# Bucket thresholds as bfloat16 masks added by TensorE and made one block later, a block-diagonal bias table, and row statistics of x from a token-major copy

## The chip, the cores and the metric

The kernel runs on one core of one Trainium2 chip. The metric is the device time of one execution, in microseconds. The engines are named as the profile names them: PE is TensorE and PEld its weight loads, DVE is VectorE, ACT is ScalarE, POOL is GpSimd, and SP is the queue engine that issues most of the DMAs.

## The reference, cut to what matters

A decoder trunk of two layers over 256 tokens with 1024 features, in float32. Layer 0 has differential attention with a relative bias, layer 1 latent attention; each has a gated FFN and a gated embedding behind it. The change touches the start of layer 0 alone:

```python
hn = rms_norm(h, attn_norm[0])                # h is x at this point
qkv = hn @ w_qkv
q = rms_norm(qkv[..., :qk_w].reshape(b, s, 8, 2, 64), q_gain)
k = rms_norm(qkv[..., qk_w:2 * qk_w].reshape(b, s, 8, 2, 64), k_gain)
...
n = max(pos_q - pos_k, 0)
log_ratio = log(max(n, 1) / 16) / log(128 / 16)
bucket = where(n < 16, n, min(16 + int(log_ratio * 16), 31))
sc = where(causal, q @ k.T * scale + rel_bias_table[bucket], -1e30)
```

The bucket of a distance n is also min(n, 16) plus the number of fifteen thresholds that n reaches. The bias of a head is a lookup in a table of 32 buckets by 8 heads.

## The kernel before, in words

All activations are feature-major: a tile holds 128 features by 256 tokens. Every matmul of float32 operands is done as three products (`mm3`, L197 to L199) of a high half and a low half. A weight unit of 128x1024 is loaded into the ring `st` (5 buffers), ScalarE casts it to the high half `wh` (L240), and VectorE or GpSimd in turn subtracts to get the low half `wl` (L241). The rings of `wh` and `wl` have 4 buffers each.

`proj_a(p)` makes q, k and v of two heads: three groups of 48 products, each with two weight units (`block`, called blocks 1 to 6 below for the two calls ahead of attention). Block 1 is `first_block`: it takes x and its weights in quarters as they land, and makes the halves of x times the norm gain (`hgH`, L637 and L639; `hgL`, L640) between its products. The norm of x itself is put in later: `epsx` adds up the squares of x over the features on ScalarE and GpSimd, `first_stats` has TensorE add them over the partitions (L301) and makes the mean `m` and its inverse root `xs["r"]`, which block 1's own normalization (`norm_block`, L342 to L353) needs.

`bias_prep` follows `first_stats` in the code, behind block 2. It builds the bias table three times in bfloat16, split so that the three add up (`tb`), in a 128x32 form with one 32x8 copy in each of four diagonal places (L401), and then the bucket index:

```python
V.tensor_scalar(bk, dist, 16.0, None, ALU.min)
for th in THRESH:
    V.scalar_tensor_tensor(bk, dist, float(th), bk, ALU.is_ge, ALU.add)
```

The index goes to memory as bfloat16 (`bkb` to `s`), and comes back as 24 loads that repeat rows of it over partitions (`oh`, L448). VectorE compares them with the partition's number (L456), and TensorE multiplies these one-hot rows with the table (`bias_mm`, 288 short products, L463). Attention starts behind that, woven with `proj_a(2)`, `proj_a(3)` and the output projection.

The order on each engine is not that of the code. The program is scheduled when it is built, by a model of time; each engine then runs its own list strictly in order and waits on semaphores. So are the loads on SP.

Of the kernel before, what the change touches and what calls it, by code (L numbers as in the profile page):

```python
# [9 lines left out]
F32 = mybir.dt.float32  # L10
# [9 lines left out]
P = 128  # L20
S = 256
# [22 lines left out]
C_LAM = 194  # L44
C_FREQ = 450
C_REL = 482
C_CONV = (490, 666)
NCONST = 842

def _out_order():  # L50
    cut = 14
# [41 lines left out]


@with_exitstack
def trunk(ctx, tc, xT, pT, pos, consts, grow, wall, out):
    nc = tc.nc
    V, A, G, T = nc.vector, nc.scalar, nc.gpsimd, nc.tensor

# [40 lines left out]
    def small(n, tag="s"):  # L140
        return sm.tile([P, 8], F32, tag=tag, name=tag, bufs=24)[:, :n]
# [161 lines left out]
        V.tensor_scalar(m, ps[:, :4].rearrange("p (a b) -> p a b", b=2)[:, :, 0], 1.0 / D, EPS, ALU.mult, ALU.add)  # L303
        return m

    def tok_stats(sq):
        m = tok_mean(sq)
        r = small(NT, "m")
        rsqrt_(r, m, NT)
        return m, r  # L310

    def rstd_diag(sq):
        m, r = tok_stats(sq)
        dg = d_tile(S)
        for t in range(NT):
            V.tensor_scalar(dg[:, t * P:(t + 1) * P], ident, r[:, t:t + 1], None, ALU.mult)
        return dg
# [71 lines left out]
    bst = {}  # L389

    def bias_prep():
        trel = col(C_REL, 8)
        tb = []
        rest = trel
        for i in range(3):
            bt = ap_.tile([P, 32], BF16, name=f"tb{i}")
            G.memset(bt, 0.0)
            q = ap_.tile([P, 8], BF16, name=f"tq{i}")
            V.tensor_copy(q, rest)
            for j in range(4):  # L400
                V.tensor_copy(bt[j * 32:(j + 1) * 32, j * 8:(j + 1) * 8], q[j * 32:(j + 1) * 32])  # L401
            tb.append(bt)
            if i < 2:
                nr = small(8)
                V.tensor_sub(nr, rest, q)
                rest = nr
        bi = ap_.tile([P, 1], F32, name="bi")
        bidx = ap_.tile([P, 1], I32, name="bidx")
        G.iota(bidx, pattern=[[0, 1]], base=0, channel_multiplier=1)
        V.tensor_scalar(bidx, bidx, 31, None, ALU.bitwise_and)  # L410
        V.tensor_copy(bi, bidx)
        V.tensor_copy(posf, posi)
        dist = e_tile()
        V.tensor_scalar(dist[:, :S], posf[:, :S], posf[:, S:S + 1], 0.0, ALU.subtract, ALU.max)
        V.tensor_scalar(dist[:, S:], posf[:, P:S], posf[:, S + 1:S + 2], 0.0, ALU.subtract, ALU.max)
        bk = e_tile()
        V.tensor_scalar(bk, dist, 16.0, None, ALU.min)
        for th in THRESH:
            V.scalar_tensor_tensor(bk, dist, float(th), bk, ALU.is_ge, ALU.add)
        bkb = ap_.tile([P, 384], BF16, name="bkb")  # L420
        V.tensor_copy(bkb, bk)
        s0 = dp.tile([P, S], BF16, name="s0")
        s1 = dp.tile([P, P], BF16, name="s1")
        nc.sync.dma_start(s0, bkb[:, :S])
        nc.sync.dma_start(s1, bkb[:, S:])
        bst["pcs"] = []
        later(LAG, lambda: bias_loads(s0, s1))
        bst["tb"], bst["bi"] = tb, bi
        ld = small(2)
        lscr = a_tile()  # L430
        for j in range(2):
            V.tensor_tensor_reduce(lscr[:, j * 64:(j + 1) * 64], col(C_LAM + 128 * j, 64),
                                   col(C_LAM + 128 * j + 64, 64), 1.0, 0.0, ALU.mult, ALU.add, ld[:, j:j + 1])
        le = small(2)
        A.activation(le, ld, AF.Exp)
        V.scalar_tensor_tensor(neglam, le[:, 1:2], -LAM_INIT, le[:, 0:1], ALU.add, ALU.subtract)
# [41 lines left out]
    def proj_a(p):  # L478
# [16 lines left out]
        for s in range(3):  # L495
# [8 lines left out]
            if p == 0 and s == 0:  # L504
                epsx()
            elif p == 0 and s == 1:
                first_stats()
                bias_prep()
            while "r" in xs and todo:
                post(*todo.pop(0))  # L510
# [114 lines left out]
                       lambda k: oL[(h0 + k) // 4][:, (h0 + k) % 4], post)  # L625

    xs = {}
    hgq = sumsq_begin()

    def get_first():  # L630

        for i in range(2):
            u = ring_pair()
            for j in range(4):
                k, q = 4 * i + j, slice(j * S, (j + 1) * S)
                if k % 2 == 0:
                    A.activation(hgH[:, k], hT[:, k], AF.Copy, scale=col(C_ATTN[0] + k))  # L637
                else:
                    V.tensor_scalar(hgH[:, k], hT[:, k], col(C_ATTN[0] + k), None, ALU.mult)  # L639
                V.scalar_tensor_tensor(hgL[:, k], hT[:, k], col(C_ATTN[0] + k), f(hgH[:, k]), ALU.mult, ALU.subtract)  # L640
                A.copy(u[0][:, q], first[i][:, q])  # L641
                V.tensor_sub(u[1][:, q], first[i][:, q], f(u[0][:, q]))
# [8 lines left out]
        return ps  # L651

    def epsx():
        for k in range(NK):
            sumsq_add(hgq, k)
        V.tensor_scalar(gq[:, 0:1], col(C_AQ), -SCALE_A, None, ALU.mult)
        V.tensor_scalar(gq[:, 1:2], col(C_QN), -SCALE_B, None, ALU.mult)
        V.tensor_scalar(gq[:, 2:3], col(C_ASUB), 1.0 - LAM_INIT, None, ALU.mult)

    def first_stats():  # L660
        m, xs["r"] = tok_stats(hgq)
        ep = cp.tile([P, 8], F32, name="epsx")
        V.tensor_scalar(ep.rearrange("p (t n) -> p t n", t=NT), m.unsqueeze(2).to_broadcast([P, NT, 4]), EPS,
                        None, ALU.mult)
# [487 lines left out]
def _layout(inp, np):  # L1152
# [96 lines left out]
    half = 32  # L1249
    arg = np.float32(-math.log(10000.0)) * np.arange(half, dtype=np.float32) * np.float32(2.0 / 64)  # L1250
    cst[:, C_FREQ:C_FREQ + half] = np.exp(arg.astype(np.float64)).astype(np.float32)
    cst[:, C_REL:C_REL + 8] = np.tile(f("rel_bias_table"), (4, 1))

    def featT(a):
        s, d = a.shape
        return np.ascontiguousarray(a.reshape(s, d // P, P).transpose(2, 1, 0))

    xT = featT(f("x")[0])
    pT = np.stack([featT(f("p")[l, 0]) for l in range(2)])
    pv = np.asarray(inp["positions"], dtype=np.int32)[0]  # L1260
    pos = np.zeros((P, S + NT), np.int32)
    pos[:, :S] = pv
    pos[:, S:] = pv.reshape(NT, P).T
    return {"in_x": xT, "in_p": pT, "in_pos": pos, "in_consts": cst, "in_grow": grow, "in_wall": wall}


# [16 lines left out]
```

## Time and profile before

| | |
|---|---|
| median of 3 runs | 793.84 us (792.4 to 794.16) |
| the profiled execution's own time | 794.75 us |
| its span, first to last instruction | 793.0 us |
| TensorE busy | 760.3 us, 96% |
| VectorE, ScalarE, GpSimd busy | 577.9, 481.6, 300.6 us |
| mean granted clock of TensorE | 0.983 of full speed |

Busy times overlap. The share of TensorE is a mean over the whole span; a stretch has to be looked at by itself to see whether TensorE or another engine sets the time there. Matmuls are pipelined, so a matmul's duration is longer than the step from one to the next.

### The profile page before, as it was taken

How to read it: one execution, taken by the hardware profiler on the slowest of the kernel's cores; microseconds unless marked ns; L12 is line 12 of the kernel's file. 1: busy time of each engine (PE TensorE's matmuls, PEld its weight loads, DVE VectorE, ACT ScalarE, POOL GpSimd, SP SyncE). 2: the span in 40 equal slices, each digit the busy share in tenths (PEclk: the TensorE clock that was granted, in tenths of full speed). 3: DMA queues.
4: the chain of work that ended last, by engine and by line, in shares of the span. 5: the costliest groups of instructions: out<-in, count | busy, mean ns of one | idle time of the engine just before them, and what ended most of it. 6: DMA issues, size and time to landing. Idle time of an engine off the chain costs nothing.

```text
span 793.0 us, 16490 instructions
## 1 busy us (share of the span) xinstructions
PE 760.3 (96%) x6384; PEld 747.9 (94%) x6384; DVE 577.9 (73%) x1158; ACT 481.6 (61%) x1039; POOL 300.6 (38%) x210
## 2 busy tenths in 40 slices
PE   6988999999999999998999899999899999999997
PEld 5877999999999999997989899999899999999997
DVE  7974888659987786547678987975558877775535
ACT  5334888567666665446866867664646666655443
POOL 5533456262333330235743746422433332301141
PEclk9989999999999999999999999999999999999999
DMA  7475345435666676555344333343455655565641
GB/s 289 158 193 185 110 132 173 133 110 184 181 191 187 188 229 206 188 167 174 112 160 136 106 107 94 99 131 108 157 157 181 194 178 181 177 194 183 185 130 54
DMA packets 37231, 126.91 MB, mean 160 GB/s; under 512 B 4640, under 2 KB 6176, under 8 KB 37152
## 3 DMA queue, kind: packets, MB, share of 16 engines
q1 hardware_dynamic: 36432, 125.32, 51.1%
q8 instruction: 50, 0.82, 0.4%
q10 hardware_dynamic: 720, 0.53, 0.2%
q14 instruction: 29, 0.24, 0.1%
HBM read 124.69 MB, written 1.15 MB: 159 GB/s over the span
## 4 chain that ended last, share of the span: by engine, by line
PE 83%; DVE 6%; issue 3%; POOL 3%; ACT 2%; DMA 2%; SPq 1%; POOLq 0%; DVEq 0%; ACTq 0%
PE pa L197 17%; PE pa L198 17%; PE pa L199 17%; PE pc L198 8%; PE pc L199 8%; PE pc L197 8%; POOL wl L241 2%; PE pb L198 1%; DVE wl L241 1%; PE pb L197 1%; PE pb L527 1%; PE pb L199 1%; PE pc L193 1%; POOL s L274 1%; PE pt L193 1%
## 5 line engine op out<-in xcount | busy, mean ns | idle before, releaser
L240 ACT CAST wh<-st 128x1024 fp32r<-128x1024 f32 x221 | 231.2, 1050 | 189.5 <-issue 70.4
L241 POOL TENSOR_TENSOR wl<-st,wh 128x1024 fp32r<-128x1024 f32 x74 | 178.4, 2411 | 240.8 <-ACT wh L240 229.4
L241 DVE TENSOR_TENSOR wl<-st,wh 128x1024 fp32r<-128x1024 f32 x147 | 189.8, 1292 | 84.3 <-ACT wh L240 83.9
L197 PE MATMUL pa<-hgH,wh 128*128 128x256 f32 x504 | 144.2, 286 | 2.2 <-ACT hgH L206 2.2
L198 PE MATMUL pa<-hgL,wh 128*128 128x256 f32 x504 | 144.2, 286 | 0.5 <-DVE hgL L207 0.3
L199 PE MATMUL pa<-hgH,wl 128*128 128x256 f32 x504 | 143.7, 285 | 0.0
L198 PE MATMUL pa<-wl,hgH 128*128 128x256 f32 x328 | 96.5, 295 | 9.5 <-DVE wl L241 6.1
L197 PEld LDWEIGHTS pa<-hgH,wh 128*128 128x128 f32 x504 | 97.9, 194 | 2.6 <-ACT hgH L206 2.6
L198 PEld LDWEIGHTS pa<-hgL,wh 128*128 128x128 f32 x504 | 97.9, 194 | 1.1 <-DVE hgL L207 1.1
L199 PEld LDWEIGHTS pa<-hgH,wl 128*128 128x128 f32 x504 | 98.0, 194 | 0.0
L197 PE MATMUL pa<-wh,hgH 128*128 128x256 f32 x328 | 95.8, 296 | 0.8 <-ACT wh L641 0.6
L199 PE MATMUL pa<-wh,hgL 128*128 128x256 f32 x328 | 95.2, 292 | 0.5 <-DVE hgL L204 0.5
L197 PE MATMUL pa<-og,wh 128*128 128x256 f32 x336 | 95.3, 287 | 0.0
L198 PE MATMUL pa<-og,wh 128*128 128x256 f32 x336 | 95.1, 284 | 0.0
L199 PE MATMUL pa<-og,wl 128*128 128x256 f32 x336 | 94.9, 283 | 0.0
L198 PE MATMUL pc<-hgL,wh 128*128 128x256 f32 x328 | 93.3, 285 | 0.6 <-DVE hgL L207 0.5
L197 PE MATMUL pc<-hgH,wh 128*128 128x256 f32 x328 | 93.5, 285 | 0.1
L199 PE MATMUL pc<-hgH,wl 128*128 128x256 f32 x328 | 93.0, 283 | 0.0
L296 POOL TENSOR_TENSOR ssq<-ssq,d 128x256 f32<-128x256 f32 x42 | 39.4, 937 | 136.5 <-ACT d L295 135.1
L198 PEld LDWEIGHTS pa<-wl,hgH 128*128 128x128 f32 x328 | 65.2, 199 | 11.1 <-DVE wl L241 6.9
L197 PEld LDWEIGHTS pa<-wh,hgH 128*128 128x128 f32 x328 | 64.4, 198 | 2.1 <-ACT wh L641 1.0
L274 POOL TENSOR_TENSOR s<-s,neghalf 128x4 f32<-128x4 f32 (+2 forms) x30 | 41.7, 1390 | 64.3 <-DVE s L345 46.1
(300 smaller groups left out, 1968.2 us busy)
## 6 DMA issues: line engine op xcount, KB each, us to landing
st<-in_wall SPq DMA_DIRECT2D x225, 512.0 KB, 3.6
oh<-s SPq DMA_DIRECT2D x24, 128.0 KB, 4.5
hT<-in_x SPq DMA_DIRECT2D x4, 256.0 KB, 5.3
st<-in_wall SPq DMA_DIRECT2D x4, 256.0 KB, 5.5
d<-in_p SPq DMA_DIRECT2D x2, 256.0 KB, 4.6
out_h<-hT SPq DMA_DIRECT2D x4, 128.0 KB, 1.9
out_h<-hT ACTq DMA_DIRECT2D x4, 128.0 KB, 2.0
grow<-in_grow SPq DMA_DIRECT2D x1, 384.0 KB, 6.1
```

Source lines behind the costliest of these rows:

```text
L193: T.transpose(o, i, ident)
L197: T.matmul(ps, lhsT=aH, rhs=bH, start=start, stop=False)
L198: T.matmul(ps, lhsT=aH, rhs=bL, start=False, stop=False)
L199: T.matmul(ps, lhsT=aL, rhs=bH, start=False, stop=stop)
L240: A.copy(hi, st)
L241: eng.tensor_sub(lo, st, f(hi))
L274: G.tensor_tensor(dst, src, neghalf[:, :n], ALU.pow)
L296: G.tensor_add(sq, sq, t)
L527: T.matmul(pss[e][:, a:b], lhsT=x[rows, j, t * P:(t + 1) * P], rhs=y[rows, j, :b - a], start=start, stop=stop)
```

## The change

Four edits at the start of layer 0:

1. The bucket index: the distance is kept in bfloat16, cut off at 128. Each threshold becomes a mask of zeros and ones in bfloat16 (ring `ge`, 4 buffers), and TensorE adds the masks up in PSUM by 16 products with an identity. ScalarE copies the sum out as the index.
2. `bias_prep` is called one block later, behind block 4 (`p == 1 and s == 0`).
3. The bias table comes from the host in its block-diagonal form of 32 columns, so that it is split by whole-tile casts and subtractions.
4. The squares of x are added up from a second copy of x, token-major (`xN`, two tiles of 512 KB through the ring `st`), by ScalarE's accumulating square. The eight squares, seven additions and the ones-product of the feature-major way go. All eight `hgH` scalings are ScalarE's now.

```diff
-    def tok_stats(sq):
-        m = tok_mean(sq)
-        r = small(NT, "m")
-        rsqrt_(r, m, NT)
-        return m, r
...
     def bias_prep():
-        trel = col(C_REL, 8)
         tb = []
-        rest = trel
+        rest = col(C_REL, 32)
         for i in range(3):
             bt = ap_.tile([P, 32], BF16, name=f"tb{i}")
-            G.memset(bt, 0.0)
-            q = ap_.tile([P, 8], BF16, name=f"tq{i}")
-            V.tensor_copy(q, rest)
-            for j in range(4):
-                V.tensor_copy(bt[j * 32:(j + 1) * 32, j * 8:(j + 1) * 8], q[j * 32:(j + 1) * 32])
+            V.tensor_copy(bt, rest)
             tb.append(bt)
             if i < 2:
-                nr = small(8)
-                V.tensor_sub(nr, rest, q)
+                nr = ap_.tile([P, 32], F32, name=f"tr{i}")
+                V.tensor_sub(nr, rest, bt)
                 rest = nr
...
-        dist = e_tile()
-        V.tensor_scalar(dist[:, :S], posf[:, :S], posf[:, S:S + 1], 0.0, ALU.subtract, ALU.max)
-        V.tensor_scalar(dist[:, S:], posf[:, P:S], posf[:, S + 1:S + 2], 0.0, ALU.subtract, ALU.max)
-        bk = e_tile()
-        V.tensor_scalar(bk, dist, 16.0, None, ALU.min)
-        for th in THRESH:
-            V.scalar_tensor_tensor(bk, dist, float(th), bk, ALU.is_ge, ALU.add)
+        identb = ap_.tile([P, P], BF16, name="identb")
+        V.tensor_copy(identb, ident)
+        dist = ap_.tile([P, 384], BF16, name="dist")
+        V.tensor_scalar(dist[:, :S], posf[:, :S], posf[:, S:S + 1], 128.0, ALU.subtract, ALU.min)
+        V.tensor_scalar(dist[:, S:], posf[:, P:S], posf[:, S + 1:S + 2], 128.0, ALU.subtract, ALU.min)
+        pb = bankB()
+        for j in range(len(THRESH) + 1):
+            ge = ap_.tile([P, 384], BF16, tag="ge", name="ge", bufs=4)
+            if j == 0:
+                V.tensor_scalar(ge, dist, 0.0, 16.0, ALU.max, ALU.min)
+            else:
+                V.tensor_scalar(ge, dist, float(THRESH[j - 1]), None, ALU.is_ge)
+            T.matmul(pb[:, :384], lhsT=identb, rhs=ge, start=j == 0, stop=j == len(THRESH))
         bkb = ap_.tile([P, 384], BF16, name="bkb")
-        V.tensor_copy(bkb, bk)
+        A.copy(bkb, pb[:, :384])
...
             elif p == 0 and s == 1:
                 first_stats()
+            elif p == 1 and s == 0:
                 bias_prep()
...
-                if k % 2 == 0:
-                    A.activation(hgH[:, k], hT[:, k], AF.Copy, scale=col(C_ATTN[0] + k))
-                else:
-                    V.tensor_scalar(hgH[:, k], hT[:, k], col(C_ATTN[0] + k), None, ALU.mult)
+                A.activation(hgH[:, k], hT[:, k], AF.Copy, scale=col(C_ATTN[0] + k))
...
     def epsx():
-        for k in range(NK):
-            sumsq_add(hgq, k)
...
     def first_stats():
-        m, xs["r"] = tok_stats(hgq)
+        xs["ss"] = small(NT, "m")
+        for t in range(NT):
+            xt = ring.tile([P, UNIT], F32, tag="st", name="st", bufs=BUF_ST)
+            nc.sync.dma_start(xt, xN[:, t])
+            A.activation(xt, xt, AF.Square, accum_out=xs["ss"][:, t:t + 1])
+        m, xs["r"] = small(NT, "m"), small(NT, "m")
+        V.tensor_scalar(m, xs["ss"], 1.0 / D, EPS, ALU.mult, ALU.add)
+        rsqrt_(xs["r"], m, NT)
```

VectorE between block 1's last low half and the fourth weight pair, before (`ex` is the distance or the running index, `wl` a low half of a weight unit, `tq` and `tb` the table):

```order
L663 TENSOR_SCALAR epsx<-m 128x8
L241 TENSOR_TENSOR wl<-st,wh 128x1024
L401 COPY tb_323<-tq_325 32x8 x4
...
L419 SCALAR_TENSOR_TENSOR ex<-ex 128x384
L343 TENSOR_REDUCE s<-d 128x8
L401 COPY tb_333<-tq_335 32x8 x4
L241 TENSOR_TENSOR wl<-st,wh 128x1024
...
L347 SCALAR_TENSOR_TENSOR s<-s,epsx 128x8
L419 SCALAR_TENSOR_TENSOR ex<-ex 128x384 x4
L241 TENSOR_TENSOR wl<-st,wh 128x1024
...
L353 TENSOR_TENSOR d<-pa,s 128x256 x2
```

And of the change, in the same place (`ge` is a mask):

```order
L338 TENSOR_REDUCE s<-d 128x8
L391 CAST tb_468<-tr_466 128x32
L415 TENSOR_SCALAR ge<-dist 128x384 x4
L241 TENSOR_TENSOR wl<-st,wh 128x1024
L415 TENSOR_SCALAR ge<-dist 128x384 x6
L659 TENSOR_SCALAR m<-m 128x2
L415 TENSOR_SCALAR ge<-dist 128x384 x2
L662 TENSOR_SCALAR epsx<-m 128x8
L342 SCALAR_TENSOR_TENSOR s<-s,epsx 128x8
L348 TENSOR_TENSOR d<-pa,s 128x256 x2
L241 TENSOR_TENSOR wl<-st,wh 128x1024
```

Although the code calls `bias_prep` a block later, the masks stand earlier: all sixteen are ahead of the second whole-unit low half, and the normalization of block 1 (L348) is one low half further ahead. TensorE, of the change, behind block 1 (its last product is the first row; `identb` is the identity):

```order
L199 MATMUL pa<-wh,hgL 128x256
L416 LDWEIGHTS identb
L416 MATMUL pb<-ge,identb 128x384
...
L197 MATMUL pa<-wh,hgH 128x256
...
L198 MATMUL pa<-wl,hgH 128x256
```

Four mask products stand behind block 1, four more behind block 2's first product, four behind its next twelve, and the last four behind its other 35. Before, none of these rows was there. ScalarE behind its first-block casts, before and of the change:

```order
L641 CAST wh<-st 128x256 x2
L240 CAST wh<-st 128x1024
L342 ACTIVATE d<-pa 128x256 x2
L240 CAST wh<-st 128x1024 x2
L435 ACTIVATE s<-s 128x2
```

```order
L635 CAST wh<-st 128x256 x2
L337 ACTIVATE d<-pa 128x256 x2
L240 CAST wh<-st 128x1024 x2
L657 ACTIVATE st,m<-st 128x1024 x2
L240 CAST wh<-st 128x1024 x2
L337 ACTIVATE d<-pa 128x512
L418 CAST bkb<-pb 128x384
```

Block 2's first cast went behind the squares of block 1's result, and the squares of x (L657) stand behind block 2's casts. SP's loads, as a difference:

```order
-L224 DMA st<-in_wall 128x1024 x4
-L669 DMA cst<-in_consts 128x352
-L817 DMA grow<-in_grow 128x768
-L224 DMA st<-in_wall 128x1024 x8
-L424 DMA s_369<-bkb 128x256
...
+L224 DMA st<-in_wall 128x1024 x2
+L656 DMA st<-in_xn 128x1024 x2
...
+L224 DMA st<-in_wall 128x1024 x6
+L421 DMA s_532<-bkb 128x256
+L422 DMA s_533<-bkb 128x128
+L224 DMA st<-in_wall 128x1024 x2
+L445 DMA oh<-s_532 32x2048 x16
```

The copy of x came in ahead of the third block's weights, and the index leaves behind eight whole units, not twelve.

## Rows read from the trace of the kernel before

**Rows 1.** Busy us of each engine by stretch, granted clock, DMA share, GB/s

```profile
0.00:80.00 80.00, 64.47 (x673) 61.34 (x674) 59.41 (x109) 34.85 (x79) 35.26 (x37) 0.91 0.65 205
80.00:160.00 80.00, 79.11 (x669) 75.76 (x667) 63.72 (x177) 60.69 (x165) 36.00 (x22) 1.00 0.44 136
```

**Rows 2.** TensorE's timeline: start, duration, instruction, idle before it and what ended it

```profile
18.66 0.58 PE L198 MATMUL pa<-wl,hgH 128*128 128x256 f32 x1 [1.62 <-DVE wl L241]
...
27.49 0.39 PE L198 MATMUL pa<-wl,hgH 128*128 128x256 f32 x1 [1.34 <-DVE wl L241]
...
43.12 0.58 PE L198 MATMUL pa<-wl,hgH 128*128 128x256 f32 x1 [2.91 <-DVE wl L241]
...
58.63 0.63 PE L193 MATMUL pt<-ident,d 128*128 128x128 f32 x4 [0.73 <-DVE d L353]
...
66.91 1.61 PE L463 MATMUL pb<-tb,oh 128*128 128x32 bf16 x58 [1.95 <-issue]
...
72.83 1.15 PE L463 MATMUL pb<-tb,oh 128*128 128x32 bf16 x38 [1.78 <-issue]
```

**Rows 3.** TensorE's timeline: two neighbouring products at 43 us, two at 57 us

```profile
43.50 0.41 PE L199 MATMUL pa<-wh,hgL 128*128 128x256 f32 x1
43.71 0.41 PE L197 MATMUL pa<-wh,hgH 128*128 128x256 f32 x1
...
57.50 0.28 PE L198 MATMUL pa<-wl,hgH 128*128 128x256 f32 x1
57.62 0.28 PE L199 MATMUL pa<-wh,hgL 128*128 128x256 f32 x1
```

**Rows 4.** VectorE's timeline

```profile
18.52 2.33 DVE L401 COPY tb<-tq 32x8 bf16<-32x8 bf16 x1
...
30.27 3.43 DVE L241 TENSOR_TENSOR wl<-st,wh 128x1024 fp32r<-128x1024 f32 x1
...
38.61 3.32 DVE L419 SCALAR_TENSOR_TENSOR ex<-ex 128x384 f32<-128x384 f32 x3
```

**Rows 5.** GpSimd's timeline

```profile
18.45 2.38 POOL L241 TENSOR_TENSOR wl<-st,wh 128x1024 fp32r<-128x1024 f32 x1 [0.48 <-ACT wh L240]
...
28.13 1.94 POOL L274 TENSOR_TENSOR s<-s,neghalf 128x8 f32<-128x8 f32 x1 [2.15 <-DVE s L347]
30.04 2.57 POOL L241 TENSOR_TENSOR wl<-st,wh 128x1024 fp32r<-128x1024 f32 x1
37.94 2.39 POOL L241 TENSOR_TENSOR wl<-st,wh 128x1024 fp32r<-128x1024 f32 x1
```

**Rows 6.** Two lines of block 1: min/median/max in ns, first and last start

```profile
L640 DVE SCALAR_TENSOR_TENSOR hgL<-hT,cst,hgH x8: 473/480/981, 4.9 to 14.2; 128x256 fp32r<-128x256 f32 x8
...
L642 DVE TENSOR_TENSOR wl<-st,wh x8: 412/416/951, 5.7 to 15.3; 128x256 fp32r<-128x256 f32 x8
```

**Rows 7.** Groups by line, first 80 us: busy us, mean ns, idle before

```profile
L419 DVE SCALAR_TENSOR_TENSOR ex<-ex 128x384 f32<-128x384 f32 x15 | 9.9, 660 | 0.2
...
L456 DVE TENSOR_SCALAR oh<-oh,bi 128x2048 bf16<-128x2048 bf16 x6 | 7.1, 1189 | 5.3 <-DMA oh<-s 5.3
...
L296 POOL TENSOR_TENSOR ssq<-ssq,d 128x256 f32<-128x256 f32 x7 | 5.7, 817 | 4.6 <-ACT d L295 4.2
...
L343 DVE TENSOR_REDUCE s<-d 128x8 f32<-128x512 f32 x4 | 2.7, 674 | 0.0
```

**Rows 8.** ScalarE's timeline

```profile
11.06 0.70 ACT L641 CAST wh<-st 128x256 fp32r<-128x256 f32 x2
...
16.78 0.66 ACT L342 ACTIVATE d<-pa 128x256 f32<-128x256 f32 x2 [3.22 <-PE pa L199]
17.32 1.99 ACT L240 CAST wh<-st 128x1024 fp32r<-128x1024 f32 x2
```

**Rows 9.** Loads into `st`, first 50 us

```profile
DMA to landing us min/median/max: 3.3/4.4/6.9
```

**Rows 10.** SP's timeline: the loads of the one-hot rows

```profile
46.99 9.76 SPq L448 DMA_DIRECT2D oh<-s  x20
```

More of the change, by code (lines that the diff above doesn't have):

```diff
@@ L46 @@
 C_REL = 482
-C_CONV = (490, 666)
-NCONST = 842
+C_CONV = (514, 690)
+NCONST = 866
 def _out_order():
@@ L95, in trunk @@
 @with_exitstack
-def trunk(ctx, tc, xT, pT, pos, consts, grow, wall, out):
+def trunk(ctx, tc, xT, xN, pT, pos, consts, grow, wall, out):
     nc = tc.nc
@@ L304, in tok_mean, with rstd_diag @@
         return m
-    def tok_stats(sq):
-        m = tok_mean(sq)
-        r = small(NT, "m")
+    def rstd_diag(sq):
+        m, r = tok_mean(sq), small(NT, "m")
         rsqrt_(r, m, NT)
-        return m, r
-    def rstd_diag(sq):
-        m, r = tok_stats(sq)
         dg = d_tile(S)
@@ L627, in trunk @@
     xs = {}
-    hgq = sumsq_begin()
     def get_first():
@@ L1251, in _layout @@
     cst[:, C_FREQ:C_FREQ + half] = np.exp(arg.astype(np.float64)).astype(np.float32)
-    cst[:, C_REL:C_REL + 8] = np.tile(f("rel_bias_table"), (4, 1))
+    for j in range(4):
+        cst[j * 32:(j + 1) * 32, C_REL + j * 8:C_REL + (j + 1) * 8] = f("rel_bias_table")
     def featT(a):
@@ L1258, in _layout @@
     xT = featT(f("x")[0])
+    xN = np.ascontiguousarray(f("x")[0].reshape(NT, P, D).transpose(1, 0, 2))
     pT = np.stack([featT(f("p")[l, 0]) for l in range(2)])
@@ L1263, in _layout @@
     pos[:, S:] = pv.reshape(NT, P).T
-    return {"in_x": xT, "in_p": pT, "in_pos": pos, "in_consts": cst, "in_grow": grow, "in_wall": wall}
+    return {"in_x": xT, "in_xn": xN, "in_p": pT, "in_pos": pos, "in_consts": cst, "in_grow": grow, "in_wall": wall}
 def kernel(**inputs):
```

## Prediction

> **What bounds the kernel now.** I read the busy time by stretch first. TensorE is busy for 79.1 of 80 us after the first 80 us, but for only 64.5 of the first 80 [rows 1]. So the time is TensorE's, and an edit at the start is worth what it takes out of TensorE's holes there. Next I read TensorE's own timeline for the pieces with idle time ahead of them [rows 2]: 1.62 us before 18.66, 1.34 before 27.49, 2.91 before 43.12, 0.73 before 58.63, then 1.95 and 1.78 before 66.91 and 72.83. All but the last three end on a low half (`wl`) written by VectorE. The hole at 43 costs twice. Products then start every 0.21 us, where they start every 0.12 us at 57.5 [rows 3]: that is the lower of the clock's two levels, after TensorE had stood still. It lasts 29 products, so 29 x 0.09 = 2.7 us more.
>
> Why is VectorE late? Its timeline [rows 4] beside GpSimd's [rows 5]: at 18.52 a 32x8 copy takes 2.33 us, at 30.27 a low half takes 3.43 us, at 38.61 three threshold steps take 3.32. Each time a 128x1024 subtraction of GpSimd (2.4 us) is under way, and VectorE goes on when it ends. The rest is the sheer work ahead of the low halves: 15 threshold steps of 0.66 us, 9.9 us in all [rows 7], and the twelve small copies.
>
> Call the 48-product groups of TensorE blocks 1 to 6 (the two first weight pairs), and the weight units u0, u1, ... (two to a block). In [rows 2] block 2 starts at 18.66, block 3 at 27.49, and the transposes behind block 6 at 58.63.
>
> **Block 1.** The change takes eight squares from ScalarE, seven additions (5.7 us) from GpSimd [rows 7], and four scalings from VectorE, which ScalarE gets. Without those additions beside them the eight `hgL` and eight `wl` steps should run at their medians, 0.48 and 0.42 us, not at up to 0.98 and 0.95 [rows 6]. ScalarE ended its last first-block cast at 11.76 [rows 8], no load waited for there, and loses about as much as it gains, so it ends near 11.6 again. VectorE follows it by half a microsecond (12.1, where it was at 15.7: the last `wl` step starts at 15.3), and block 1 ends near 13.0 where it ended just ahead of the wait at 17.0.
>
> **Block 2.** In the new order ScalarE casts u2 and u3 only behind the squares of block 1: 13.0 + 0.55 + 1.0 + 1.0, so u2 is there at 14.6 and u3 at 15.6 [rows 8]. VectorE has meanwhile the reduction (0.67) [rows 7] and eight masks. A mask is a bfloat16 step of 384 columns, which the trace lacks. The one bfloat16 step that it has takes 1.19 us on the mean for 2048 columns [rows 7], with waits in it; by columns that is 0.22 us, and the threshold step that it replaces took 0.66. I take 0.2, nearer to the row of its own type. So u2's low half runs from 15.4 to 16.6 and block 2 starts there, 2 us earlier. The first eight mask products lie in TensorE's wait before it and cost nothing; without that wait they would cost 8 x 0.18 (384 columns at 0.12 us for 256 [rows 3]), 1.4 us. GpSimd's u3 comes right behind VectorE's u2 and holds VectorE to about 19.0; masks 9 to 12 follow, and TensorE waits for both near 20.
>
> **Block 3.** The statistics of x now come from two 512 KB loads and two squares of 128x1024 on ScalarE. I price a square as the cast of that shape, 1.0 us [rows 8] (bounds 1.0 and, with the accumulator read, 1.3): done near 18, hidden behind block 2. The loads stand third and fourth in SP's weight stream and take two of the five `st` buffers, so u4 is issued at 12.2, when u1's buffer is free, and lands 4.4 us later (3.3 to 6.9) [rows 9], at 16.6 to 19: still ahead of use. Behind a late copy of x ScalarE's casts of u4 and u5 would wait. The block-diagonal table is three casts and two subtractions of 32 columns in place of twelve copies, under half a microsecond in the same place, and its 24 more columns of constants are 12 KB. Then the last masks, the powers on GpSimd (the 128x8 one 1.94 us [rows 5]) to about 22.6, and there u5's half on GpSimd goes first (2.4), so that VectorE has u4's low half at 25.0 + 1.2. Block 3 starts at 26.3, 1.2 us earlier than before. The last four mask products and the first transposes end before that.
>
> **Blocks 3 to 6** are the large term. Before, they took 58.63 - 27.49 = 31.1 us. VectorE now has no threshold step left there, and the low halves of u6 and u8 fall due at 32 and 38 while VectorE can give them at 28 and 32. Products alone: 191 x 0.12 = 22.9, and 0.6 for one group of transposes, 23.5. That removes 7.6: the holes of 2.91 and 0.73, the 2.7 of clock, the rest smaller. The bucket index is ready near 26, where the threshold steps alone ended at 41.9 [rows 4]. SP then has u10 and u11, 20 loads of the one-hot rows, u12 and four more. These took 9.8 us to issue [rows 10], so they end near 41, before the transposes at 49.8; u12 is not needed before 52. What is queued behind the index on SP, u10 and u11, is due at 43.
>
> **The bias products and attention** stand in the same order as before, so I give them the same time. Sum: 1.2 + 7.6 = 8.8 us. The profiled execution took 794.75 (793.0 of it span), 0.91 above the median 793.84. So 785.95 in a like execution, and **785.0** as a median.
>
> [...] The rows above show VectorE held for as long as a subtraction of GpSimd lasts, by copies and two-input steps alike [rows 4, 5]. [...] With VectorE first at u2 the sum stands at 785.0; with GpSimd first it is the first rival's 786.4.
>
> **Rivals.** (1) *GpSimd first.* u2 and u3 are free for it within 0.2 us of each other. If GpSimd takes u3 at 15.4, VectorE's u2 ends at 19.0, block 2 starts no earlier than before, and block 3 at 27.7: 1.4 us more, 786.4. If TensorE then stands long enough for the slow products to come back as at 43, 2.7 more, 789.1. For it: the margin; against: VectorE's queue is back to back there. The same times result if a mask costs 0.66: 8 x 0.46 = 3.7, 788.7.
> (2) *The holes at 66.91 and 72.83 go too.* They end on nothing that the trace shows, in the middle of a run of short bias products. They are 3.7 us, and the slow products behind the second (9 x 0.09) 0.8: 780.5. For it: their place is not tied to any data. Against: the same short products run at the same rate, so I expect them again. [...]
> (3) *No change.* The time is given back in attention because VectorE or ScalarE bounds it: 793.8. Against: TensorE at 79.1 of 80 there, VectorE 63.7, ScalarE 60.7 [rows 1].
> (4) *Slower.* TensorE's queue is in order, and now holds four groups of four mask products among its own. If VectorE's masks wait for GpSimd at each group, a group costs 2.4 us of hole and 2.7 of slow clock, 5.1. Two groups take 10.2 and only eat the 8.8 (795.2, no change that can be measured); from three on the kernel is slower (800.3), and four give 805. Against: the first eight masks are made before GpSimd has anything to do, and the last group has block 2's last 35 products ahead of it.
>
> **How the numbers follow.** Forecast 0.57 (782.5 to 786), (1) 0.22 (786 to 789.5), (2) 0.10 (780 to 782.5), (3) 0.06 (within 0.2%, 1.6 us, which is about what a measurement of this kernel can tell from no change), (4) 0.05. Faster: 0.57 + 0.22 + 0.10 = 0.89; same 0.06; slower 0.05. The range takes the forecast and the first rival and the edge of the second: 782.0 to 789.5.
>
> **What would show it.** Right: block 1 ends near 13, block 2 starts at 16 to 17, block 3 near 26, no hole over 1 us from there to the transposes near 50, the granted clock full in that stretch, the index copy near 26, and everything from the bias products on 8 to 9 us earlier. Wrong: a GpSimd subtraction starting ahead of VectorE's u2; slow products after 26; TensorE waiting on a mask with VectorE idle; a ScalarE cast waiting for u4's or u5's load behind the copy of x; or the gain present at 50 us and gone at 160.

## The result, and the profile after

The changed kernel took 786.44 us (median of 5 runs, 783.85 to 789.36), the kernel before 793.84 (5 runs, 792.4 to 795.85). The ratio is 0.9897, with a 95% interval of 0.9874 to 0.992: faster by 7.4 us where 8.8 were forecast. The profiled execution is the slowest of the five, 789.36 us, 787.6 of it span. First the windows that answer to [rows 1], and three inside the first 80 us (busy us of TensorE, its weight loads, VectorE, ScalarE and GpSimd, then granted clock, DMA share, GB/s).

```profile
0.00:80.00 80.00, 70.43 (x744) 66.86 (x745) 48.04 (x116) 43.23 (x99) 34.71 (x29) 0.96 0.73 231
80.00:160.00 80.00, 78.67 (x669) 75.64 (x668) 62.59 (x165) 61.62 (x166) 38.06 (x26) 1.00 0.43 128
...
20.00:40.00 20.00, 20.00 (x166) 19.71 (x166) 10.76 (x24) 11.05 (x16) 12.44 (x7) 1.00 0.89 253
40.00:60.00 20.00, 14.41 (x188) 14.33 (x187) 15.12 (x18) 7.44 (x16) 10.60 (x5) 0.85 0.91 277
60.00:80.00 20.00, 20.00 (x304) 18.83 (x304) 8.98 (x29) 12.04 (x41) 6.21 (x4) 0.97 0.26 83
```

The whole gain is in the first 80 us: TensorE is 6.0 us busier there, and from 80 to 160 it is as busy as before. From 20 to 40 it does not stand at all; the stretch from 40 to 60 is the odd one. TensorE's timeline of the changed kernel shows why (it answers to [rows 2]; the row at 48.88 is the one that stood at 58.63):

```profile
15.32 0.39 PE L197 MATMUL pa<-wh,hgH 128*128 128x256 f32 x1 [0.78 <-ACT wh L240]
...
17.00 0.39 PE L198 MATMUL pa<-wl,hgH 128*128 128x256 f32 x1 [0.63 <-DVE wl L241]
...
19.91 0.39 PE L198 MATMUL pa<-wl,hgH 128*128 128x256 f32 x1 [0.55 <-POOL wl L241]
...
48.88 0.60 PE L193 MATMUL pt<-ident,d 128*128 128x128 f32 x4
49.31 2.55 PE L460 MATMUL pb<-tb,oh 128*128 128x32 bf16 x96
57.45 0.55 PE L197 MATMUL pa<-wh,hgH 128*128 128x256 f32 x1 [5.58 <-DVE d L348]
...
68.95 0.95 PE L525 MATMUL pb<-qk 64*128 64x128 f32 x6
```

At 48.88 the gain is 9.75 us. Then there is a new hole, 5.58 us ahead of block 7's first product, and the products behind it step by 0.21 us until 60.8, as in [rows 3] behind the hole at 43: 16 steps, 1.4 us. The granted clock is 0.50 in both stretches (57.45 to 60.80 here, 43.12 to 49.20 before the change) and 1.00 where the step is 0.12 us (57 to 58 before the change); the clock records of both traces hold no other value. The two holes of [rows 2] that ended on "issue" (1.95 and 1.78 us), and the slow products behind them, are gone. 9.75 - 5.58 - 1.4 + 3.7 + 0.8 is 7.3. GpSimd's step on the two row statistics at the end of layer 0 and near the end of the program tells what arrives. Before the change:

```profile
173.02 0.71 POOL L274 TENSOR_TENSOR m<-m,neghalf 128x2 f32<-128x2 f32 x1 [0.25 <-DVE m L303]
...
773.43 0.70 POOL L274 TENSOR_TENSOR m<-m,neghalf 128x2 f32<-128x2 f32 x1
```

And after it:

```profile
165.57 0.71 POOL L274 TENSOR_TENSOR m<-m,neghalf 128x2 f32<-128x2 f32 x1
...
768.03 0.71 POOL L274 TENSOR_TENSOR m<-m,neghalf 128x2 f32<-128x2 f32 x1
```

7.45 us at 165, 5.4 at the end. This one execution lost 2 us in between, in two places, both at a lower clock: some 0.95 us between 356 and 396 (the granted clock from 360 to 400 was 0.91, where the kernel before had 0.96 in the stretch that answers to it), and 1.2 us between 451 and 458 (0.79 from 450 to 458, where the kernel before had 1.00).

Now the new hole, followed backwards. VectorE's list, GpSimd's, ScalarE's and SP's in the changed kernel:

```profile
50.05 0.75 DVE L453 TENSOR_SCALAR oh<-oh,bi 128x2048 bf16<-128x2048 bf16 x1
50.72 0.68 DVE L338 TENSOR_REDUCE s<-d 128x8 f32<-128x512 f32 x1
51.43 0.17 DVE L342 SCALAR_TENSOR_TENSOR s<-s,epsx 128x8 f32<-128x8 f32 x1
53.40 3.31 DVE L241 TENSOR_TENSOR wl<-st,wh 128x1024 fp32r<-128x1024 f32 x1 [1.80 <-ACT wh L240]
56.63 0.68 DVE L348 TENSOR_TENSOR d<-pa,s 128x512 f32<-128x512 f32 x1
```

```profile
51.67 1.64 POOL L274 TENSOR_TENSOR s<-s,neghalf 128x8 f32<-128x8 f32 x1 [3.91 <-DVE s L342]
53.27 5.65 POOL L241 TENSOR_TENSOR wl<-st,wh 128x1024 fp32r<-128x1024 f32 x2
```

```profile
47.76 1.05 ACT L240 CAST wh<-st 128x1024 fp32r<-128x1024 f32 x1 [8.40 <-DMA st<-in_wall]
48.72 0.59 ACT L337 ACTIVATE d<-pa 128x512 f32<-128x512 f32 x1
51.03 1.05 ACT L240 CAST wh<-st 128x1024 fp32r<-128x1024 f32 x1 [1.73 <-DMA st<-in_wall]
```

```profile
28.80 12.75 SPq L445 DMA_DIRECT2D oh<-s  x20
41.70 0.35 SPq L224 DMA_DIRECT2D st<-in_wall  x1
42.27 1.81 SPq L445 DMA_DIRECT2D oh<-s  x4
44.30 14.98 SPq L224 DMA_DIRECT2D st<-in_wall  x8
```

Block 7 waits for a PSUM bank: the one that held block 5's sums, which are read by ScalarE's square (L337 at 48.72), and then by VectorE's scaling (L348 at 56.63). The square stands in ScalarE's in-order list behind the cast of u12, and that cast waited 8.40 us for its load; block 5's last product had started at 43.00. SP could issue u12 only behind 20 loads of the one-hot rows, at 41.70, and it landed at 47.7. The square late, the reduction and the power are late, and by then the next low half stands ahead of L348 on VectorE (53.40, 3.31 us beside GpSimd's pair). So a DMA queue reaches TensorE over three in-order lists. Block 7's second unit is late as well: u13 was issued at 44.30, its cast starts at 51.03, and its low half is the first of GpSimd's pair, which by itself took 2.35 us, to 55.6. Block 7 has 12 products ahead of that, 1.4 us; so without the wait for the bank TensorE would still stand some 2.3 us, from 53.3 to 55.6 (an estimate from these rows).

### The profile page after: what moved, and what is told of

The parts are those of the page before. It is cut to its first block, busy times and chain, and to the rows that moved or that the text cites. A ratio compares the mean times of both kernels' runs of the same rounds, so it can differ in the third digit from the quotient of the medians.

```text
span 787.6 us, 16504 instructions
## 1 busy us (share of the span) xinstructions
PE 761.2 (97%) x6396; PEld 748.7 (95%) x6396; DVE 561.2 (71%) x1142; ACT 483.8 (61%) x1040; POOL 296.0 (38%) x200
## 4 chain that ended last, share of the span: by engine, by line
PE 83%; DVE 6%; DMA 4%; ACT 3%; POOL 2%; issue 2%; SPq 0%; POOLq 0%; ACTq 0%; DVEq 0%
PE pa L197 17%; PE pa L198 17%; PE pa L199 17%; PE pc L198 8%; PE pc L199 8%; PE pc L197 8%; DMA oh<-s 2%; DMA st<-in_wall 1%; POOL wl L241 1%; PE pb L198 1%; DVE wl L241 1%; PE pb L197 1%; PE pc L193 1%; PE pb L199 1%; PE pb L525 1%
## 5 line engine op out<-in xcount | busy, mean ns | idle before, releaser
L241 POOL TENSOR_TENSOR wl<-st,wh 128x1024 fp32r<-128x1024 f32 x74 | 180.4, 2438 | 245.8 <-ACT wh L240 226.3
L296 POOL TENSOR_TENSOR ssq<-ssq,d 128x256 f32<-128x256 f32 x35 | 33.6, 961 | 132.2 <-ACT d L295 131.7
L199 PEld LDWEIGHTS pa<-wh,hgL 128*128 128x128 f32 x328 | 64.6, 197 | 0.8 <-DVE hgL L204 0.7
```

What stands on the lines that cost most here:

```text
L199: T.matmul(ps, lhsT=aL, rhs=bH, start=False, stop=stop)
L241: eng.tensor_sub(lo, st, f(hi))
L296: G.tensor_add(sq, sq, t)
```

## Experiments

All medians in one table; the kernel before, run beside them, took 793.1 to 793.9 us. Most differences below are of a few us, and the intervals are some 2 us wide to either side, so the readings rest on the traces as well.

| version | median us | ratio to before, 95% interval |
|---|---|---|
| the change | 786.44 | 0.9897 [0.9874, 0.992] |
| later place alone | 791.92 | 0.9977 [0.9958, 0.9996] |
| index edit alone (masks, table, place) | 789.59 | 0.996 [0.9933, 0.9987] |
| statistics alone | 787.24 | 0.9916 [0.9886, 0.9945] |
| change without masks | 787.07 | 0.9933 [0.991, 0.9956] |
| change, two weight units ahead | 787.14 | 0.9919 [0.9891, 0.9948] |
| change, block 7 from another pool | 787.08 | 0.993 [0.9903, 0.9957] |
| change, 4 of 24 one-hot loads | 782.98 | 0.9865 [0.9837, 0.9893] |
| change, six wide loads (4 x 32) | 801.32 | 1.0097 [1.0073, 1.0121] |
| the same and the other pool | 801.22 | 1.0106 [1.0082, 1.013] |
| **change, six wide loads (32 x 4)** | **780.23** | 0.9835 [0.9812, 0.9858] |
| that without masks | 784.3 | 0.9879 [0.9856, 0.9901] |
| that without the statistics edit | 786.04 | 0.9887 [0.986, 0.9913] |

**The parts, one at a time.** The index edit alone leaves the statistics as they were:

```diff
+        for k in range(NK):
+            sumsq_add(hgq, k)
...
-        xs["ss"] = small(NT, "m")
-        for t in range(NT):
-            xt = ring.tile([P, UNIT], F32, tag="st", name="st", bufs=BUF_ST)
...
+        m, xs["r"] = tok_stats(hgq)
```

> The change without its statistics: masks on TensorE, the later place and the block-diagonal table, but the squares of x are added up from the feature-major tile as before, and VectorE scales every other hgH as before. Theory A (the gain is VectorE's: fifteen threshold steps no longer stand ahead of the low halves of blocks 3 to 6, and the statistics only shorten block 1): the hole of 2.9 us near 43 and the slow products behind it are gone, the time is 786 to 789.5. Rival B (the gain comes from the statistics, which free GpSimd and give block 1's normalization early): 791 to 794, the hole near 43 stays.

The other way round, the kernel before with the statistics edit alone:

```diff
-        m, xs["r"] = tok_stats(hgq)
+        xs["ss"] = small(NT, "m")
+        for t in range(NT):
+            xt = ring.tile([P, UNIT], F32, tag="st", name="st", bufs=BUF_ST)
+            nc.sync.dma_start(xt, xN[:, t])
+            A.activation(xt, xt, AF.Square, accum_out=xs["ss"][:, t:t + 1])
```

> The kernel before with the statistics alone: row sums of squares from the token-major copy on ScalarE, all hgH scalings on ScalarE; index, table and place as before. Theory A: block 1 ends near 13.7 as in the change, but the threshold steps still stand ahead of the low halves, so a hole of 2 us or more with slow products behind it stays before 50 us, and the time is 789.5 to 793. Rival B: 785 to 788.

And the kernel before with the later place alone:

```diff
             elif p == 0 and s == 1:
                 first_stats()
+            elif p == 1 and s == 0:
                 bias_prep()
```

> The kernel before with one edit: bias_prep is called behind block 4 and not behind block 2. Theory A: the same VectorE steps, only moved towards the low halves of blocks 3 to 6, so 791 to 797. Rival E (the place is what helps: block 1's normalization and the low halves go ahead of the index): 785.5 to 789.

Measured: gains of 4.3, 6.7 and 2.0 us. Index edit and statistics together should give 11.0 and give 7.4. The theory that the statistics alone are worth little fell, and the index edit's time lies 0.1 us above the range that was expected (its ten executions spread from 787.1 to 794.2). TensorE's holes behind block 4, in the three profiles in this order:

```profile
57.00 2.10 PE L465 MATMUL pb<-tb,oh 128*128 128x32 bf16 x72 [2.70 <-DVE oh L458]
...
69.31 1.68 PE L465 MATMUL pb<-tb,oh 128*128 128x32 bf16 x53 [2.02 <-issue]
```

```profile
48.03 0.39 PE L197 MATMUL pa<-wh,hgH 128*128 128x256 f32 x1 [3.02 <-DVE qk L207]
```

```profile
48.03 0.41 PE L197 MATMUL pa<-wh,hgH 128*128 128x256 f32 x1 [3.14 <-DVE qk L207]
...
62.86 0.55 PE L197 MATMUL pa<-wh,hgH 128*128 128x256 f32 x1 [4.50 <-DVE d L353]
```

Each version has a hole of its own between 45 and 63, near its one-hot loads, wherever the early part ended. Something there takes back what the early part gains.

The index edit also needs the statistics edit. Each version's lists are built anew, and without the statistics edit they hold the last masks back: in the index edit alone VectorE's last two masks stand at 40.37, and SP's first store of the index at 44.13, no earlier than before the change (43.47). In the change it is at 25.58. So the worth of a part, here and below, is that of the edit with the lists that it brings.

**The masks alone.** The changed kernel with VectorE's old chain of thresholds:

```diff
...
-            if j == 0:
-                V.tensor_scalar(ge, dist, 0.0, 16.0, ALU.max, ALU.min)
-            else:
-                V.tensor_scalar(ge, dist, float(THRESH[j - 1]), None, ALU.is_ge)
-            T.matmul(pb[:, :384], lhsT=identb, rhs=ge, start=j == 0, stop=j == len(THRESH))
...
+        for th in THRESH:
+            V.scalar_tensor_tensor(bk, dist, float(th), bk, ALU.is_ge, ALU.add)
...
```

> The changed kernel with the old way to the index: VectorE's chain of float32 compare-and-add over the thresholds and VectorE's copy to bf16, in place of the bf16 masks summed by TensorE; its later place, the block-diagonal table and the token-major statistics are kept. Theory M, the masks carry their own share: the chain's fifteen or so instructions of VectorE delay the normalizations and weight splits of blocks 2 to 4, TensorE idles 2 to 5 us more there, and the time is 789 to 792. Rival N, the statistics alone made room and the chain now fits into VectorE's idle time, while the later index only moves the one-hot loads: the time is 785.5 to 788.5, no different from the changed kernel.

787.07: rival N, no difference. Yet its early part is worse, and its one-hot loads go out 7 us later:

```profile
18.36 0.39 PE L198 MATMUL pa<-wl,hgH 128*128 128x256 f32 x1 [1.93 <-POOL wl L241]
...
24.07 0.39 PE L198 MATMUL pa<-wl,hgH 128*128 128x256 f32 x1 [1.13 <-DVE wl L241]
...
56.75 0.55 PE L197 MATMUL pa<-wh,hgH 128*128 128x256 f32 x1 [3.74 <-DVE d L348]
```

Block 7 starts at 56.75 where it started at 57.45 with the masks. What came earlier in the changed kernel waited longer.

**What makes the hole.** First two weight units' loads were written ahead of the one-hot loads, and taken from there later:

```diff
+        return split_unit(ahead.pop(0) if ahead else next(fetch()))
...
+        ahead.extend(next(fetch()) for _ in range(2))
```

> The change, with the loads of the weight units u12 and u13 written ahead of the one-hot loads, so that SP issues them among these (u12 behind 8 of 24, u13 behind 16). Theory C (the hole of 5.6 us at 51.9 to 57.4 in the change is the weight units that SP issues behind the one-hot loads, whose casts ScalarE waits 8.4 and 1.7 us for): the hole falls under 1.5 us and the time is 779 to 783; if the two holes inside the bias products, which the change has lost, come back with it, 783 to 784.5. Rival D (GpSimd's two subtractions holding VectorE there make the hole, the loads are only near): the hole stays over 3.5 us and the time is 785 to 788.

787.14. The time is in the rival's range, but its cause does not show: the low half ahead of the scaling (L350 here) took 1.22 us at 54.51 and is not held by GpSimd. The built order put u12 behind 8 one-hot loads and u13 behind 16, so u12's cast came 4.6 us earlier, and u13's, which now stands ahead of the square, as late as u12's had been:

```profile
43.19 1.05 ACT L240 CAST wh<-st 128x1024 fp32r<-128x1024 f32 x1 [3.90 <-DMA st<-in_wall]
47.99 1.05 ACT L240 CAST wh<-st 128x1024 fp32r<-128x1024 f32 x1 [3.76 <-DMA st<-in_wall]
48.95 0.59 ACT L339 ACTIVATE d<-pa 128x512 f32<-128x512 f32 x1
```

Ahead of the scaling two compares of one-hot rows waited for their loads as well (1.32 us at 49.90 and 1.01 at 53.84). TensorE's hole is 4.68 us:

```profile
56.47 0.55 PE L197 MATMUL pa<-wh,hgH 128*128 128x256 f32 x1 [4.68 <-ACT wh L240]
```

The cast that the row names is that of a later unit and ended at 56.34, the scaling at 56.32; which of the two released TensorE, the trace cannot tell. So this version moved the lateness from u12 to u13, and leaves open what loads ahead of all the one-hot loads would give.

Next, block 7's sums from another pool:

```diff
-                ps = bankA()
+                ps = bankC() if (p, s) == (2, 0) else bankA()
```

> The changed kernel with block 7's sums in another PSUM bank than the one that VectorE's normalization of pass 1's k frees at 57.31. Theory P, the hole of 5.58 us is the wait for that bank alone: block 7 starts as soon as its weights are there, TensorE's idle time between 51.87 and 57.45 falls below 2.5 us, attention starts 2.5 to 4 us earlier and the time is 782.5 to 784.5. Rival Q, the weights of block 7 are late as well (ScalarE's cast of u13 ended near 52, the next at 53.6, GpSimd's two splits end at 58.9): the idle time moves to the weight splits, a few products start earlier and wait in the middle of the block, the sum of the idle times stays above 4 us and the time is 785 to 788.

787.08, hole 4.54 us with the same releaser. This tells nothing of theory P: in the built program the tile has the other pool's name and stands in bank 0 again, where block 5's sums were (the trace shows the name and the releaser, not the bank). A different bank for block 7 was not tried.

Then the loads themselves, first with one DMA for the four pieces of a tile:

```diff
-                for j in range(4):
-                    nc.sync.dma_start(oh[j * 32:(j + 1) * 32], row[j:j + 1].broadcast_to([32, ipp, nq]))
+                nc.sync.dma_start(oh, row.unsqueeze(1).broadcast_to([4, 32, ipp, nq]))
```

> The changed kernel with each one-hot source tile loaded by one DMA of 128 partitions (6 of 512 KB) in place of four DMAs of 32 partitions (24 of 128 KB, of which the changed kernel's trace shows 20 taking 12.75 us of SP's issue, 28.80 to 41.55, while all DMA moved 220 to 250 GB/s at a share of 0.87 to 0.99). Theory F, the narrow loads starve the weight units: with six issues the weight units u12 and u13 land some 5 us earlier, ScalarE's squares for block 5 are no longer behind a late cast, and TensorE's hole of 5.58 us at 51.87 to 57.45 shrinks below 2 us; the first product of the attention comes at 63.5 to 66 (68.95 in the changed kernel) and the time is 780 to 783, or up to 784.5 if the two idle times that end with an instruction issue (1.95 and 1.78 us before the change) come back. Rival G, the 3.1 MB themselves are the limit, however they are cut: the DMA share stays near 0.9 for some 12 us after the first issue, the hole stays within 1.5 us of its size, and the time is 785 to 788.

And the same with the other pool:

> The changed kernel with both edits: one-hot source tiles by six DMAs of 128 partitions, and block 7's sums in another PSUM bank. If both theories (F and P) hold, no idle time above 1 us stands between 20 and 60 us and the time is 778 to 782. If the narrow loads are the whole cause it equals the version with wide loads alone within 1 us. If neither holds (rivals G and Q) it is 785 to 788.

801.32 and 801.22, slower than before by 1%: a miss for both theories. A window inside these loads, and the same for the changed kernel's (the columns are those of the first windows):

```profile
32.00:44.00 12.00, 11.03 (x93) 10.82 (x91) 3.11 (x7) 4.71 (x7) 5.15 (x2) 1.00 0.26 106
```

```profile
30.00:41.00 11.00, 11.00 (x95) 11.00 (x94) 5.00 (x6) 6.58 (x9) 5.66 (x3) 1.00 0.92 236
```

The DMA share is 0.26 in the first, 4.2 of the 16 engines on the mean, at 106 GB/s; the weight units queue behind them (the five issued from 44 to 60 us took 25.0 us to land, where the changed kernel's took 5.8, both medians), and TensorE stood 16.74 us ahead of 69.27. That says how the loads are cut matters much, and gave two more versions. One leaves out 20 of the 24 loads (all six compares read one tile, so the bias is not the reference's):

```diff
+                if not bst["pcs"]:
+                    raw = act.tile([P, ipp, nq], BF16, tag="og", name="raw", bufs=8)
...
-                V.tensor_scalar(oh, oh, bi, None, ALU.is_equal)
+                V.tensor_scalar(oh, src, bi, None, ALU.is_equal)
```

> The changed kernel with 4 of the 24 one-hot source loads: one tile is loaded, and all six compares read it and write tiles of their own, so the other 20 loads (2.6 MB) are left out and the bias is not the reference's; every other instruction stays. Theory F, the one-hot loads hold the weight units u12 to u15 back, and everything behind them: TensorE's hole of 5.58 us at 51.87 to 57.45 falls below 1.5 us, the first product of the attention comes at 62.5 to 65.5 (68.95 in the changed kernel) and the time is 779.5 to 783.5. Rival I, the hole comes from the order of the lists on ScalarE and VectorE and from the PSUM bank, whatever the DMA does: hole within 1.5 us of its size, 785.5 to 788.

The other reads the source as 32 repeats of 4 rows, with the table and the compare values laid out to match:

```diff
-                for j in range(4):
-                    nc.sync.dma_start(oh[j * 32:(j + 1) * 32], row[j:j + 1].broadcast_to([32, ipp, nq]))
+                nc.sync.dma_start(oh, row.unsqueeze(0).broadcast_to([32, 4, ipp, nq]))
...
-        V.tensor_scalar(bidx, bidx, 31, None, ALU.bitwise_and)
+        V.tensor_scalar(bidx, bidx, 2, None, ALU.logical_shift_right)
...
-        cst[j * 32:(j + 1) * 32, C_REL + j * 8:C_REL + (j + 1) * 8] = f("rel_bias_table")
+        cst[j:P:4, C_REL + j * 8:C_REL + (j + 1) * 8] = f("rel_bias_table")
```

> The changed kernel with the one-hot tiles loaded by 6 DMAs of 128 partitions (512 KB) as in the version with wide loads, but with the source read as 32 repeats of 4 rows in place of 4 rows of 32 repeats; the table's rows and the compare values are laid out for that order of partitions, the result is the same. The version with wide loads showed a DMA share of 0.25 and 104 GB/s while its loads ran, as if each ran on 4 of the 16 DMA engines. Theory J, a load is spread over the engines by the outermost step of its source, 4 there and 32 here: the share stays above 0.8 at 350 to 420 GB/s, all the loads are done 8 to 9 us after the first issue (about 14 in the changed kernel), the hole shrinks to 0 to 2.5 us, and the time is 780.5 to 784.5. Rival K, the engines are chosen in some other way, and six loads of 512 KB again run on few of them: share below 0.5, hole above 8 us, time above 790. Rival G as before, 3.1 MB cost the same however they are cut: 785.5 to 788.

With 20 loads left out: 782.98, and block 7's hole is 1.06 us. Theory F holds, though attention's first product, at 65.72, is 0.2 us behind its range. A hole of 1.25 us at 44.84 is left: the six compares, all ready at once, run ahead of a low half that is due:

```profile
37.44 6.21 DVE L457 TENSOR_SCALAR oh<-raw,bi 128x2048 bf16<-128x2048 bf16 x6 [2.53 <-DMA raw<-s]
```

With all the data in six loads of the second kind: 780.23, the fastest of all, just below theory J's range (and 344 GB/s from 28 to 42, just below the rate that it gave). SP's list, the window from 40 to 60, and the first products of attention (68.95 in the changed kernel):

```profile
28.24 4.13 SPq L444 DMA_DIRECT2D oh<-s  x6
```

```profile
40.00:60.00 20.00, 20.00 (x395) 19.93 (x394) 12.08 (x15) 10.73 (x32) 12.61 (x6) 1.00 0.68 247
```

```profile
60.69 0.95 PE L524 MATMUL pb<-qk 64*128 64x128 f32 x6
```

No hole of half a microsecond stands between 20 and 60 us, and the clock is full there. Attention starts 8.3 us earlier than in the changed kernel. The same 3.1 MB move; it was not their amount.

**The parts again, with the loads out of the way.** The six-load version without the masks, and without the statistics edit (both edits as above):

> The version with six loads, without the masks: the index comes from VectorE's old chain, as in the version without masks, which took the same time as the changed kernel while the one-hot loads held both back. Theory R, the masks were worth something all along and the late stretch took it back: the chain's idle times of TensorE (1.93 and 1.13 us at 18.36 and 24.07, beside 0.63 and 0.55 in the changed kernel) and the index's later arrival (the first store of it at 33.4 instead of 25.6, with the one-hot loads 7 us later) now reach the end: 782.5 to 786. Rival N, the masks are worth nothing here: 779 to 781.5.

> The version with six loads, without the statistics edit: x's squares and their column sums on TensorE stay as before the change. Theory R, with the loads no longer the limit, each edit keeps its own share: the statistics, worth 2 to 3 us beside the index edit while the narrow loads ran (789.6 against 786.4 to 787.1), are now worth 3 to 7, and the time is 783.5 to 787. Rival S, the index edit and the loads alone carry the gain, and the statistics' earlier start of blocks 2 to 4 is given back in idle time elsewhere: 779.5 to 782.5.

784.3 and 786.04: theory R both times. The masks are worth 4.1 us here (0.6 with the narrow loads), the statistics 5.8 (3.2 with them). These are differences of medians. The row statistic at the end of layer 0, in the profiled executions, says the same: without the masks it comes at 165.41 (165.57 with them) beside the narrow loads, but at 162.87 (157.76 with them) beside the six; without the statistics edit at 169.82 and 165.93. The hole ahead of block 7 is back without the masks, for the index then leaves later (its first store at 33.16, 25.02 with them):

```profile
23.80 0.39 PE L198 MATMUL pa<-wl,hgH 128*128 128x256 f32 x1 [1.25 <-DVE wl L241]
...
55.40 0.35 PE L197 MATMUL pa<-wh,hgH 128*128 128x256 f32 x1 [2.39 <-DVE d L348]
```

So the parts are real, and the narrow loads hid a share of each.

## Why the prediction was right, and where a step of it failed

**Block 1, block 2.** The squares of block 1 start at 13.68 (13.0 forecast) and block 2 at 17.00 (16.6). VectorE's u2 came first, as the forecast had it and rival 1 did not: GpSimd's subtraction started 0.6 us behind and paid for it, 3.56 us in place of 2.4.

```profile
15.73 1.22 DVE L241 TENSOR_TENSOR wl<-st,wh 128x1024 fp32r<-128x1024 f32 x1
```

```profile
16.30 3.56 POOL L241 TENSOR_TENSOR wl<-st,wh 128x1024 fp32r<-128x1024 f32 x1 [13.76 <-PE pb L416]
```

The price of a mask, chosen at 0.2 us, and the square of x, at 1.0 with 1.3 as its bound:

```profile
L415 DVE TENSOR_SCALAR ge<-dist x15: 247/253/1068, 12.9 to 20.3; 128x384 bf16<-128x384 bf16 x15
```

```profile
16.10 1.07 ACT L657 ACTIVATE st<-st 128x1024 f32<-128x1024 f32 x1
17.06 0.20 ACT L657 ACTIVATION_READ_ACCUMULATOR st<-st 128x1 f32 x1
```

A mask is 0.25 us alone and four of them took 0.76. The square and its read took 1.06 together (the next square starts at 17.16). Both choices held. The longest mask, 1.07 us, stands in the row at 18.91 below and began while GpSimd's subtraction was under way (16.30 to 19.86); in the index edit alone one took 2.47 us beside another subtraction. So the masks are not free of GpSimd either, though the four at 16.86 ran at their usual pace beside its start:

```profile
18.91 1.24 DVE L415 TENSOR_SCALAR ge<-dist 128x384 bf16<-128x384 bf16 x2 [1.28 <-PE pb L416]
```

**Block 3.** It starts at 25.35, 0.95 us ahead of the 26.3 forecast. The forecast had GpSimd's half of u5 go first and hold VectorE's u4. It came behind: u5's cast waited for TensorE until 22.97, GpSimd began at 24.49, and VectorE had begun u4 a microsecond before.

```profile
23.45 1.22 DVE L241 TENSOR_TENSOR wl<-st,wh 128x1024 fp32r<-128x1024 f32 x1
...
25.35 0.37 PE L198 MATMUL pa<-wl,hgH 128*128 128x256 f32 x1
```

**Blocks 3 to 6.** They took 23.53 us, 23.5 forecast. At the transposes behind block 6 the gain was to be 8.8 us and is 9.75, and block 3's start is all of the difference. The holes of 2.91 and 0.73 us and the slow clock are gone, and no hole over 0.6 us is left from 20 to 49, with the clock at 1.00 from 20 to 40. The index copy stands at 25.07 (26 forecast), and the 20 one-hot loads end at 41.55 (41 forecast). Two signs of being wrong did show. ScalarE's cast of u4 waited 1.01 us at 19.31 for its load behind the copy of x; no hole of TensorE ends on that cast. And slow products came after 26, behind the new hole.

**The step that failed** is "The bias products and attention stand in the same order as before, so I give them the same time", with its ground that u12 is not needed before 52. For u12 itself that ground was right: its cast ended at 48.8. Two things were left out. The cast stands in a list: ScalarE's square for block 5 is behind it, and block 7's PSUM bank behind that. That cost 5.58 us of hole and 1.4 of slow clock. And u13, issued behind the last one-hot loads, is due 1.4 us after block 7's first possible start and would by itself have come 2.3 us late. The forecast came near the time nonetheless, because the second rival's gain came too: the two holes that ended on "issue", 3.7 us, and 0.8 of slow products behind them. -7.0 and +4.5, with 0.95 more than forecast ahead of them, leave 1.5 us of loss, near the 1.4 us by which 785.0 was too low. So the last term, given as nothing, was two large ones of opposite sign, and that the number came so near is luck.

The narrow loads' share of it is shown by the six-load version, which moves the same data and has neither hole nor slow clock. That it is the PSUM bank on which block 7 stood is read from the built program and from the releaser in the trace; no version with another bank was run.

**The rivals.** (1) did not happen. (2) happened, beside the hole; what the traces show of these two holes is told in the last section. (3) is excluded by 7.45 us of gain at 165. (4) did not happen: VectorE waited once for TensorE's mask products (1.28 us at 18.91), TensorE for no mask.

## What to carry to other kernels

When an edit brings a stretch forward, follow the next shared queue, not only the next consumer: read which in-order list the late instruction stands in, and what else is queued behind it there. An edit that measures as worthless may only be hidden behind another limit, so measure it again once that limit is gone (the masks: 0.6 us, then 4.1). Of a broadcast load, check which dimension is outermost in its source, for that decided between 801 and 780 us here.

## What the runs showed of the hardware

The same 512 KB tile, loaded with its source as 4 rows of 32 repeats, kept 0.26 of the DMA engines busy at 106 GB/s; as 32 repeats of 4 rows it did not hold the rest back, and from 28 to 42 us, these loads and weight units together, 344 GB/s moved:

```profile
DMA packets 1313, 4.81 MB, mean 344 GB/s; under 512 B 141, under 2 KB 141, under 8 KB 1312
```

The changed kernel moved 243 GB/s from 28 to 42. Both fit theory J: a share of 0.26 is 4.2 of 16 engines where the outermost step of the source is 4, and with 32 there the loads and weight units took 0.94 of the 16 engines' time from 28 to 42. No one-hot load with another step was run, so how the engines of a load are chosen is not shown beyond these two.

The narrow loads had a cost of their own here. While the changed kernel's loads of 32 partitions ran, the DMA share was 0.92 and yet only 236 GB/s moved. The packets of that window:

```profile
DMA packets 897, 2.60 MB, mean 236 GB/s; under 512 B 266, under 2 KB 266, under 8 KB 896
```

The trace has a time for each packet. The 266 small ones, of 4 bytes each, took 3.7 us in all; the 630 of 4 KB took 157.3 us, 0.25 us each. Before the change, from 47 to 57 us beside the same narrow loads, a 4 KB packet took 0.26 us. In the version with six wide loads (4 x 32), at its share of 0.26, it took 0.16 us (25 GB/s to an engine, from 106 GB/s and 4.2), and in the six-load version from 28 to 42 us 0.18. So the time went into the data packets, which were slower beside the narrow loads, and not into the small ones; why they are slower, no run here shows.

The holes that end on "issue" stood in the kernel before (1.95 and 1.78 us), in the index edit alone (2.02) and in its six-load version (1.08); the version with six wide loads (4 x 32) has a short one (0.29 us, to 80.78), and the other ten have none, the later place alone among these. The traces place them. The one that ends at 72.83 before the change, and the three of the other versions, all end after TensorE has started 1217 instructions, matmuls and weight loads counted together; the one that ends at 66.91 comes after 961, just 256 fewer. And a packet of 16 KB on a queue that the page of the profile names "q8 instruction" had ended 1.39 to 1.55 us before the end of each of the five:

| version | packet ended | hole ended |
|---|---|---|
| before, after 961 | 65.47 | 66.91 |
| before, after 1217 | 71.31 | 72.83 |
| index edit alone | 67.92 | 69.31 |
| six loads, without the statistics edit | 62.14 | 63.58 |
| six wide loads (4 x 32) | 79.23 | 80.78 |

In the ten versions that pass count 1217 without a hole, the packet had ended 1.5 us or more before that point (2.34 us in the changed kernel, 64.05 to 66.39). So in all fourteen traces the holes fit a wait for that packet. That TensorE waits there for its own instructions is the author's reading of these times: what the packet holds is not shown, no version was made to move one of the holes, and why the packet comes late in some versions is not shown either.
